# Batched x·yᵀ in float32: tile 0 leaves PSUM in two separate halves, loads and tiles take other slots, and tiles 2 to 5 leave as pairs

## The chip, the cores and the metric

The kernel runs on one core of one Trainium2 chip. The metric is the device time of one execution in microseconds (us); the kernel before has a median of 297.6 us over three runs (297.5 to 297.63). Engines are called PE (matrix products), DVE (VectorE), ACT (ScalarE), POOL (GpSimd) and SP (SyncE, which here only issues transfers). Transfers between HBM and on-chip memory (SBUF) are moved by 16 DMA engines.

## The reference

```python
def setup_inputs():
    batch, n_heads, seq_t, seq_s, channels = 8, 12, 512, 512, 64
    ...
def reference(x, y):
    return np.einsum('bhtc,bhsc->bhts', x, y).astype(np.float32)
```

For each of the 96 heads, a 512 x 64 matrix times a transposed 512 x 64 matrix gives a 512 x 512 matrix. The inputs are 25.2 MB and the output is 100.7 MB, all float32.

## The kernel before

**Tiles.** The 96 heads form six groups of 16. A *load* brings one group of x or of y, 2 MB, into one slot of SBUF: 128 partitions by 16 KB. There are twelve loads; load n is x of group n/2 for even n and y for odd n. A *result tile* is two heads of output, also 2 MB and also one slot; there are 48, four to each half group. The buffer `room` holds eight slots. Loads use slots 0 to 4; slots 5 to 7 at first hold bf16 copies of groups 1 to 3 and serve as result slots once these have been used.

**Stages.** `compress(n)` turns a landed load into bf16: an x load by one ACT cast of about 3.6 us; a y load by four casts of quarters, two on DVE, one on POOL, one on ACT (for the last y load none on ACT). `mix` (POOL for the first three half groups, DVE later) puts x in a layout padded with zeros, and `transposes` (DVE) makes the operands xT and yT of a half group. PE then computes a tile as two *halves*, each four matmuls into one of two PSUM buffers `pm0` and `pm1`; ACT copies each half from PSUM into the tile's slot ("evicts" it, 128 x 2048 values), which frees that PSUM buffer for PE. When both halves are in the slot, SP issues the store to HBM.

**Order.** The order on each engine is that of the program, written by hand in the loop over n at line 430 and the loop over tiles at line 446. Every engine works strictly through its own list, and `emit` puts the semaphore waits in front of each instruction. SP's list matters here: it holds all loads and stores, so a load or store behind a waiting one waits too. Loads 0 to 4 are issued first, loads 5 to 9 after `compress(0..4)`, load 10 after `compress(6)` and load 11 after `compress(8)`. `result(o)` (line 390) evicts the two halves of tile o and calls `store(o)` (line 365). Tile 0 comes after `compress(8)`, tile 1 after `compress(9)`, tile 2 after `compress(10)`, tile 3 before `compress(11)`, and the others after the loop.

**Slots and stores.** Line 154 (`places`) gives the slot of each load, line 155 (`alone`) that of the first six tiles (`SINGLE`), which are stored one by one at line 382: 2 MB each, read as 16 KB from each partition. From tile 6 on, two tiles lie in adjacent slots and are stored by one transfer of 4 MB at line 386, read as 32 KB from each partition. `ROUNDS` lists which pair of slots each such store uses: three pairs in turn for the first ten, then four. The last four tiles have a special arrangement (`shares`, `rest`): part of tile 44 is stored in small pieces, some of them from POOL's queue, and a part of it is computed again at the very end.

**Waits on a slot.** A tile may be evicted into a slot once the previous store from it has landed, or, for a slot that held a load, once all casts have read it. Slots 5 to 7 also wait for the readers of the bf16 copies there (`held`).

Of the kernel before, what the change touches and what calls it, by code (L numbers as in the profile page):

```python
# [9 lines left out]
def kernel(  # L10
# [25 lines left out]
    NH = 2 * NG  # L36
    V = G // 4
    K = 8
# [1 line left out]
    D = 32  # L40
    SLOTS = 5
    N = K * S
    SINGLE = 2 * V - 2
    SHARED = V * NH - V
    PAIRS = 4
    LATE = 10
    ROUND = [1, 0, 2]
    ROUNDS = [ROUND[n % 3] for n in range(LATE)]
    while len(ROUNDS) < (V * NH - SINGLE) // 2:
        ROUNDS += [PAIRS - 1, *ROUND[LATE % 3:], *ROUND[:LATE % 3]]  # L50
    LAST = 2 * ROUNDS[(V * NH - SINGLE) // 2 - 1]
    CUT = [S, 3 * S]
    LEFT = 2 * S
    fp32 = mybir.dt.float32
# [8 lines left out]
    ov = of.rearrange("(o u h q n) -> o h q u n", u=2, h=V, q=Q * E, n=N)  # L63
    ow = of.rearrange("(o a j q n) -> o j q a n", a=4, j=2, q=Q * E, n=N)

    def buffer(name, width, dtype):
        return nc.alloc_sbuf_tensor(name, [P, width], dtype)[:, :]

    room = buffer("room", 2 * PAIRS * N, fp32)
    pairs = [room[:, 2 * n * N:2 * (n + 1) * N] for n in range(PAIRS)]  # L70
    slots = [p[:, j * N:(j + 1) * N] for p in pairs for j in range(2)]

    def spare(g, lo, hi):

# [24 lines left out]
    def need(name, points, told=True):  # L99

        best = {}
        for p, v in points:
            if known[name].get(p, 0) < v:
                best[p] = max(best.get(p, 0), v)
        for p, v in list(best.items()):
            if any(snaps[q, w].get(p, 0) >= v for q, w in best.items() if q != p):
                del best[p]
        for p, v in best.items():
            if told:
                engines[name].wait_ge(sems[p], v)  # L110
            known[name][p] = v
            for q, w in snaps[p, v].items():
                known[name][q] = max(known[name].get(q, 0), w)
# [20 lines left out]
    def signal(p):  # L134
        if p not in sems:
            sems[p] = nc.alloc_semaphore(p)
        return sems[p]

    def emit(name, make, reads=(), writes=(), dma=None, by=None, step=1):
        need(name, promise(name, reads, writes))  # L140
        p = by or name
        if dma is not None:
            p, step = f"dma{dma}", 16
        made = make().then_inc(signal(p), step)
        record(name, p, step, reads, writes, dma is not None)
        return made.ins.name


    late = [f"dma{LAST}", "dmapool"]
    for p in late:  # L150
        signal(p)
    loaded = {}

    places = [0, 1, 2, 3, 4, 0, 1, 2, 3, 4, 1, 3]
    alone = [0, 2, 4, 0, 1, 4]
    heads = [0, 2, 1, 3]
    held = {
        SLOTS + g - 1: [[("xk", g)], [("yb", h, g, ch) for h in range(2) for ch in range(2)]]
# [15 lines left out]
    def both(*ids):  # L174
        return [("slot", i, pm) for i in ids for pm in range(2)]

    def place(ap, pattern):
        name = ap.tensor.name
        return mybir.PhysicalAccessPattern(
            ap=pattern, offset=ap.offset, dtype=ap.dtype, memref=name, memsetref=f"{name}_set"  # L180
        )

    def transfer(name, dst, src, to=None, of=None):

        to = to or dst.ap
        of = of or [src.ap[0], *[[1, 1]] * (len(to) - len(src.ap)), *src.ap[1:]]
        return engines[name].add_instruction(  # L187
            mybir.InstDMACopy(
                name=nc.get_next_instruction_name(),
                engine=engines[name].engine,  # L190
                ins=[place(src, of)],
                outs=[place(dst, to)],
                mode="Copy",
                cce_op=mybir.AluOpType.bypass,
                queue={"sp": "qSPDynamicHW", "pool": "qPoolDynamic"}[name],
            )
        )
# [48 lines left out]
    def transposes(i):  # L246
        g, half = divmod(i, 2)
        b = g % (NG - 1 + half)
        emit(
            "dve",  # L250
            lambda: nc.vector.transpose(  # L251
                xTs[half].rearrange("p (k r e) -> p k e r", k=K, e=E),
                xbs[half].rearrange("p (k e c) -> p k e c", k=K, e=E),
            ),
            [("xb", half, part) for part in range(4)],
            [("xT", half)],
        )
        emit(
            "dve",
            lambda: nc.vector.transpose(  # L260
                yTs[half].rearrange("p (r j) -> p j r", r=D),
                ybs[half][b].rearrange("p (j c) -> p j c", c=D),
            ),
            [("yb", half, b, ch) for ch in range(2)],
            [("yT", half)],
            by="made",
            step=V,
        )
# [23 lines left out]
    def part(name, dst, src, k, reads, dma):  # L292

        assert src.ap[0][1] == 2 * k and dst.ap[0][1] == k
        emit(
            name, lambda: transfer(name, dst, src, dst.ap),
            reads=reads, dma=dma,
        )

    def shares(o, s):  # L300

        to, mine = ov[o // V, heads[o % V]], slots[s]
        def odd(name, b, e, k, lo, hi):

            p = 4 * e + 32 * b + (32 if e > 7 else 0)
            n = 2 * k
            dst = to[p // 2:p // 2 + n, 1, lo:hi].rearrange("(k i) n -> k i n", i=2)
            part(name, dst, mine[p + 1:p + 2 * n:2, lo:hi], k, both(s), "pool" if name == "pool" else s)

        for b in range(2):  # L310
            for e, k in turns:
                odd("pool", b, e, k, 0, N if e else CUT[b])
        for b in range(2):
            odd("sp", b, 0, 4, CUT[b], N - b * LEFT)
# [35 lines left out]
    def rest():  # L350
# [7 lines left out]
        for b, first, width, n, e, k, skip in sorted(remade, key=lambda r: r[4]):  # L358
# [3 lines left out]
            p = lies(e)  # L362
            part("pool", dst, mine[p + 1:p + 4 * k:2, skip:skip + width], k, [("xk", 0)], "pool")

    def store(o):
        i, j = divmod(o, V)
        if o == SHARED:
            s = 2 * ROUNDS[(o - SINGLE) // 2]
            shares(o, s)
        elif o == SHARED + 1:  # L370
            n = ROUNDS[(o - SINGLE) // 2]
            emit(
                "sp", lambda: transfer("sp", ow[i, heads[j - 1]][:, :2], pairs[n][::2]),
                reads=both(2 * n, 2 * n + 1), dma=2 * n,
            )
            emit(
                "sp", lambda: transfer("sp", ov[i, heads[j]][:, 1], slots[2 * n + 1][1::2]),
                reads=both(2 * n + 1), dma=2 * n + 1,
            )
        elif o < SINGLE:  # L380
            s = alone[o]
            emit("sp", lambda: nc.sync.dma_start(ov[i, heads[j]], slots[s]), reads=both(s), dma=s)
        elif o % 2:
            n = ROUNDS[(o - SINGLE) // 2]
            emit(
                "sp", lambda: transfer("sp", ow[i, heads[j - 1]], pairs[n]),
                reads=both(2 * n, 2 * n + 1), dma=2 * n,
            )

    def result(o):  # L390

        s = alone[o] if o < SINGLE else 2 * ROUNDS[(o - SINGLE) // 2] + o % 2
        ot = slots[s].rearrange("p (r s) -> p r s", s=S)
        for k in range(0, K, 4):
            pm = k // 4
            half = o // V % 2
            reads, writes = [("xT", half), ("yT", half)], [("pm", pm)]
            signal("pe")
            need("pe", promise("pe", reads, writes), told=False)
            record("pe", "pe", 1, reads, writes)  # L400
            copy(
                "dve" if o == V * NH - 1 else "act", ot[:, k:k + 4, :], pms[pm],
                [("pm", pm)], [("slot", s, pm), *(held[s][pm] if s in held else ())], by=f"free{pm}",
            )
        store(o)

    def prepare(i):

        if i < NH:
            transposes(i)  # L410
        if i + 1 < NH:
            for part in range(4):
                mix(i + 1, "dve", part)
# [14 lines left out]
            writes=[("xb", half, part) for part in range(4)],  # L428
        )
    for n in range(2 * NG):  # L430
        if n == 11:
            result(3)
        compress(n)
        mix(n // 4, "pool", n % 4)
        if n == 4:
            transposes(0)
        if n < 5:
            load(n + SLOTS)
        elif n in (6, 8):
            load(n // 2 + 7)  # L440
        if n > 7 and n < 11:
            result(n - 8)
        if n == 9:
            transposes(1)
    prepare(2)
    for o in range(V, V * NH):
        result(o)
        if o % V == V - 1:
            prepare(o // V + 2)
# [39 lines left out]
```

## Time and profile before

The median is 297.6 us. The profiled execution took 297.78 us, of which the core's span from first to last instruction is 296.0 us; 1.78 us lie around it.

| view | value |
|---|---|
| DMA, hardware queue, share of 16 engines over the span | 98.7% |
| bytes moved, mean rate | 125.85 MB, 425 GB/s |
| ACT busy | 205.2 us (69%) |
| DVE busy | 157.5 us (53%) |
| PE busy | 138.5 us (47%) |
| POOL busy | 64.7 us (22%) |
| ACT, eviction of half a tile | 1.89 us each, 94 of them |
| ACT, cast of an x load | 3.62 us |
| ACT, cast of a quarter of a y load | 2.45 us |
| single store, 2048 KB, issue to landing | 11.0 us median |
| pair store, 4096 KB, issue to landing | 24.3 us median |

The time from issue to landing counts the time that a transfer stands behind earlier ones in the queue. An engine's idle time costs the kernel nothing while the DMA engines have work; what costs is a moment in which the queue of transfers is empty.

### The profile page before, as it was taken

How to read it: one execution, taken by the hardware profiler on the slowest of the kernel's cores; microseconds unless marked ns; L12 is line 12 of the kernel's file. 1: busy time of each engine (PE TensorE's matmuls, PEld its weight loads, DVE VectorE, ACT ScalarE, POOL GpSimd, SP SyncE). 2: the span in 40 equal slices, each digit the busy share in tenths (PEclk: the TensorE clock that was granted, in tenths of full speed). 3: DMA queues.
4: the chain of work that ended last, by engine and by line, in shares of the span. 5: the costliest groups of instructions: out<-in, count | busy, mean ns of one | idle time of the engine just before them, and what ended most of it. 6: DMA issues, size and time to landing. Idle time of an engine off the chain costs nothing.

```text
span 296.0 us, 1222 instructions
## 1 busy us (share of the span) xinstructions
PE 138.5 (47%) x403; PEld 37.6 (13%) x403; DVE 157.5 (53%) x76; ACT 205.2 (69%) x106; POOL 64.7 (22%) x33
## 2 busy tenths in 40 slices
PE   0000040558576556557644856567646646674000
PEld 0000010112121111111111211111111111121000
DVE  2257897996969591925908568772925100052000
ACT  1665676999799979666966999969666976640000
POOL 2399989996000000000000000000000000402000
PEclk9999995556779995778789599975798786757555
DMA  7999999999999999999999999999999999999998
GB/s 283 425 432 430 427 432 427 432 427 430 430 434 447 425 426 443 438 443 443 425 425 422 425 425 438 447 434 443 430 425 425 425 425 434 424 424 453 409 422 354
DMA packets 6042, 125.85 MB, mean 425 GB/s; under 512 B 952, under 2 KB 952, under 8 KB 996
## 3 DMA queue, kind: packets, MB, share of 16 engines
q1 hardware_dynamic: 5656, 124.95, 98.7%
q0 software_dynamic: 384, 0.89, 0.8%
q14 instruction: 2, 0.02, 0.0%
HBM read 25.17 MB, written 100.66 MB: 425 GB/s over the span
## 4 chain that ended last, share of the span: by engine, by line
DMA 52%; ACT 25%; PE 6%; issue 5%; DVE 3%; POOL 1%; SPq 0%; ACTq 0%
DMA out_dram<-room 38%; ACT room L166 24%; DMA room<-in_y_dram 7%; DMA room<-in_x_dram 6%; PE pm L274 4%; DVE room L168 3%; PE pm L343 2%; ACT xk L166 1%; ACT yb L166 1%; POOL out_dram L187 1%; DVE xk L168 0%; SPq L203 0%; ACTq L110 0%
## 5 line engine op out<-in xcount | busy, mean ns | idle before, releaser
L274 PE MATMUL pm<-yT,xT 128*128 128x512 bf16 x384 | 133.6, 492 | 130.6 <-ACT room L166 93.9
L166 ACT ACTIVATE room<-pm 128x2048 f32<-128x2048 f32 x94 | 170.1, 1891 | 35.0 <-DMA out_dram<-room 31.8
L251 DVE STREAM_TRANSPOSE xT<-xb 128x2048 uint32<-128x2048 uint32 x12 | 46.7, 3895 | 59.6 <-PE pm L274 54.9
L274 PEld LDWEIGHTS pm<-yT,xT 128*128 128x128 bf16 x384 | 35.3, 113 | 228.0 <-ACT room L166 148.2
L187 POOL DMA_DIRECT2D out_dram<-room x6 | 3.5, 590 | 180.8 <-ACT room L166 180.8
L168 DVE COPY xb<-room 32x2048 bf16<-32x2048 bf16 x20 | 26.1, 1304 | 0.6
L166 ACT ACTIVATE room<-room 128x4096 bf16<-128x4096 f32 (+1 forms) x6 | 18.2, 3039 | 11.1 <-DMA room<-in_x_dram 7.3
L168 POOL COPY xb<-xk 32x2048 bf16<-32x2048 bf16 x8 | 23.5, 2937 | 6.7 <-ACT xk L166 6.3
L168 DVE CAST yb<-room 64x2048 bf16<-64x2048 f32 x6 | 17.1, 2853 | 9.5 <-DMA room<-in_y_dram 9.5
L168 DVE COPY room<-pm 128x2048 f32<-128x2048 f32 x2 | 4.5, 2286 | 31.9 <-PE pm L274 31.9
L168 DVE CAST room<-room 64x2048 bf16<-64x2048 f32 x6 | 19.0, 3170 | 4.1 <-DMA room<-in_y_dram 4.0
L168 DVE COPY xb<-xk 32x2048 bf16<-32x2048 bf16 x16 | 20.9, 1304 | 0.4
L166 ACT ACTIVATE xk<-room 128x4096 bf16<-128x4096 f32 x3 | 10.8, 3617 | 5.5 <-DMA room<-in_x_dram 5.4
L168 POOL CAST yb<-room 64x2048 bf16<-64x2048 f32 x4 | 12.8, 3188 | 0.5 <-DMA room<-in_y_dram 0.2
L168 POOL COPY xb<-room 32x2048 bf16<-32x2048 bf16 x4 | 12.7, 3180 | 0.3
L260 DVE STREAM_TRANSPOSE yT<-yb 128x1024 uint32<-128x1024 uint32 x6 | 11.6, 1940 | 0.0
L260 DVE STREAM_TRANSPOSE yT<-room 128x1024 uint32<-128x1024 uint32 x6 | 11.4, 1906 | 0.0
L168 POOL CAST room<-room 64x2048 bf16<-64x2048 f32 x3 | 8.5, 2837 | 1.0 <-DMA room<-in_y_dram 0.7
L166 ACT ACTIVATE yb<-room 64x2048 bf16<-64x2048 f32 x2 | 4.9, 2454 | 1.3 <-DMA room<-in_y_dram 1.3
L343 PE MATMUL pm<-yT,xT 128*84 128x512 bf16 (+17 forms) x19 | 5.0, 442 | 0.6 <-DVE room L168 0.6
L187 POOL DMA_DIRECT2D out_dram<-xk x3 | 1.7, 571 | 15.2 <-DVE xk L168 15.2
L427 DVE MEMSET xb<- 128x2048 uint32 x1 | 1.8, 1765 | 4.5 <-PEq L419 4.5
(8 smaller groups left out, 7.0 us busy)
## 6 DMA issues: line engine op xcount, KB each, us to landing
out_dram<-room SPq DMA_DIRECT2D x20, 4096.0 KB, 24.3
out_dram<-room SPq DMA_DIRECT2D x7, 2048.0 KB, 11.0
room<-in_x_dram SPq DMA_DIRECT2D x6, 2048.0 KB, 18.6
room<-in_y_dram SPq DMA_DIRECT2D x6, 2048.0 KB, 20.8
out_dram<-room SPq DMA_DIRECT2D x1, 1024.0 KB, 29.4
out_dram<-room POOLq DMA_DIRECT2D x2, 256.0 KB, 18.4
out_dram<-room POOLq DMA_DIRECT2D x2, 96.0 KB, 16.4
out_dram<-room SPq DMA_DIRECT2D x1, 112.0 KB
```

What stands on the lines that cost most here:

```text
L166: lambda: nc.scalar.activation(dst, src, COPY)
L168: else engines[name].tensor_copy(dst, src),
L187: return engines[name].add_instruction(mybir.InstDMACopy(name=nc.get_next_instruction_name(), engine=engines[name].engine, ins=[place(src, ...
L251: lambda: nc.vector.transpose(xTs[half].rearrange("p (k r e) -> p k e r", k=K, e=E), xbs[half].rearrange("p (k e c) -> p k e c", k=K, e=E),),
L260: lambda: nc.vector.transpose(yTs[half].rearrange("p (r j) -> p j r", r=D), ybs[half][b].rearrange("p (j c) -> p j c", c=D),),
L274: last = nc.tensor.matmul(pms[k // 4][:, j, :], xT[:, k + j, h, :], yT[:, h * S:(h + 1) * S], start=True, stop=True,)
L343: last = nc.tensor.matmul(pms[0][:top, at // S, at % S:at % S + hi - lo], xT[:, stop - top:stop], yT[:, h * S + lo % S:h * S + lo % S + hi ...
L427: lambda: engines[name].memset(xbs[half], 0.0),
```

## The change

- **Tile 0 in halves.** `result` is split: `evict(o, ...)` copies the named halves, and `result` calls it for both and then `store`. Half 0 of tile 0 is now evicted before ACT's cast of `compress(7)` and half 1 after it. Its store is issued after `compress(8)` and load 11. Tile 1 follows at once after `compress(8)`, and tiles 2 and 3 both after `compress(10)`.
- **Slots.** Loads and tiles get other slots. For the loads this is a renaming (slot 1 becomes 3, 2 becomes 1, 3 becomes 2). `home(o)` gives a tile's slot: tiles 0 and 1 in slots 0 and 1, the pairs then from the list `FIRST` of first slots: 3, 0, 2, then 4, 0, 2 repeated, then 6, 4, 0, 2 repeated.
- **Pairs.** `SINGLE` falls from 6 to 2, so tiles 2 and 3 leave as one store of 4 MB, and tiles 4 and 5 as another. There are 28 large stores (tiles 0 and 1, and pairs) where there were 30, before the special arrangement of tiles 44 and 45. Tiles 26 and 27 are the first in slots 6 and 7, as before.

```diff
-    SINGLE = 2 * V - 2
+    SINGLE = 2
...
-    LATE = 10
-    ROUND = [1, 0, 2]
-    ROUNDS = [ROUND[n % 3] for n in range(LATE)]
-    while len(ROUNDS) < (V * NH - SINGLE) // 2:
-        ROUNDS += [PAIRS - 1, *ROUND[LATE % 3:], *ROUND[:LATE % 3]]
-    LAST = 2 * ROUNDS[(V * NH - SINGLE) // 2 - 1]
+    LATE = 12
+    FIRST = [3, 0, 2, *[4, 0, 2] * 3]
+    while len(FIRST) < (V * NH - SINGLE) // 2:
+        FIRST += [6, 4, 0, 2]
+    LAST = FIRST[(V * NH - SINGLE) // 2 - 1]
...
-    places = [0, 1, 2, 3, 4, 0, 1, 2, 3, 4, 1, 3]
-    alone = [0, 2, 4, 0, 1, 4]
+    places = [0, 3, 1, 2, 4, 0, 3, 1, 2, 4, 3, 2]
...
+    def home(o):
+        return o if o < SINGLE else FIRST[(o - SINGLE) // 2] + o % 2
+
     def store(o):
         i, j = divmod(o, V)
+        s = home(o)
+        pair = room[:, (s - 1) * N:(s + 1) * N]
...
         elif o < SINGLE:
-            s = alone[o]
             emit("sp", lambda: nc.sync.dma_start(ov[i, heads[j]], slots[s]), reads=both(s), dma=s)
         elif o % 2:
-            n = ROUNDS[(o - SINGLE) // 2]
             emit(
-                "sp", lambda: transfer("sp", ow[i, heads[j - 1]], pairs[n]),
-                reads=both(2 * n, 2 * n + 1), dma=2 * n,
+                "sp", lambda: transfer("sp", ow[i, heads[j - 1]], pair),
+                reads=both(s - 1, s), dma=s - 1,
             )
-    def result(o):
-        s = alone[o] if o < SINGLE else 2 * ROUNDS[(o - SINGLE) // 2] + o % 2
+    def evict(o, *pms_of):
+        s = home(o)
         ot = slots[s].rearrange("p (r s) -> p r s", s=S)
-        for k in range(0, K, 4):
-            pm = k // 4
+        for pm in pms_of:
+            k = 4 * pm
...
+    def result(o):
+        evict(o, 0, 1)
         store(o)
...
     for n in range(2 * NG):
-        if n == 11:
-            result(3)
+        if n == 7:
+            evict(0, 0)
         compress(n)
         mix(n // 4, "pool", n % 4)
...
-        if n > 7 and n < 11:
-            result(n - 8)
-        if n == 9:
+        if n == 7:
+            evict(0, 1)
+        elif n == 8:
+            store(0)
+            result(1)
+        elif n == 9:
             transposes(1)
+        elif n == 10:
+            result(2)
+            result(3)
```

More of the change, by code (lines that the diff above doesn't have):

```diff
@@ L42 @@
     N = K * S
-    SINGLE = 2 * V - 2
+    SINGLE = 2
     SHARED = V * NH - V
     PAIRS = 4
-    LATE = 10
-    ROUND = [1, 0, 2]
-    ROUNDS = [ROUND[n % 3] for n in range(LATE)]
-    while len(ROUNDS) < (V * NH - SINGLE) // 2:
-        ROUNDS += [PAIRS - 1, *ROUND[LATE % 3:], *ROUND[:LATE % 3]]
-    LAST = 2 * ROUNDS[(V * NH - SINGLE) // 2 - 1]
+    LATE = 12
+    FIRST = [3, 0, 2, *[4, 0, 2] * 3]
+    assert len(FIRST) == LATE
+    while len(FIRST) < (V * NH - SINGLE) // 2:
+        FIRST += [6, 4, 0, 2]
+    LAST = FIRST[(V * NH - SINGLE) // 2 - 1]
     CUT = [S, 3 * S]
@@ L69 @@
     room = buffer("room", 2 * PAIRS * N, fp32)
-    pairs = [room[:, 2 * n * N:2 * (n + 1) * N] for n in range(PAIRS)]
-    slots = [p[:, j * N:(j + 1) * N] for p in pairs for j in range(2)]
+    slots = [room[:, n * N:(n + 1) * N] for n in range(2 * PAIRS)]
     def spare(g, lo, hi):
@@ L363, in rest @@
             part("pool", dst, mine[p + 1:p + 4 * k:2, skip:skip + width], k, [("xk", 0)], "pool")
+    def home(o):
+        return o if o < SINGLE else FIRST[(o - SINGLE) // 2] + o % 2
     def store(o):
         i, j = divmod(o, V)
+        s = home(o)
+        pair = room[:, (s - 1) * N:(s + 1) * N]
         if o == SHARED:
-            s = 2 * ROUNDS[(o - SINGLE) // 2]
             shares(o, s)
         elif o == SHARED + 1:
-            n = ROUNDS[(o - SINGLE) // 2]
             emit(
-                "sp", lambda: transfer("sp", ow[i, heads[j - 1]][:, :2], pairs[n][::2]),
-                reads=both(2 * n, 2 * n + 1), dma=2 * n,
+                "sp", lambda: transfer("sp", ow[i, heads[j - 1]][:, :2], pair[::2]),
+                reads=both(s - 1, s), dma=s - 1,
             )
             emit(
-                "sp", lambda: transfer("sp", ov[i, heads[j]][:, 1], slots[2 * n + 1][1::2]),
-                reads=both(2 * n + 1), dma=2 * n + 1,
+                "sp", lambda: transfer("sp", ov[i, heads[j]][:, 1], slots[s][1::2]),
+                reads=both(s), dma=s,
             )
         elif o < SINGLE:
-            s = alone[o]
             emit("sp", lambda: nc.sync.dma_start(ov[i, heads[j]], slots[s]), reads=both(s), dma=s)
         elif o % 2:
-            n = ROUNDS[(o - SINGLE) // 2]
             emit(
-                "sp", lambda: transfer("sp", ow[i, heads[j - 1]], pairs[n]),
-                reads=both(2 * n, 2 * n + 1), dma=2 * n,
-            )
-    def result(o):
-        s = alone[o] if o < SINGLE else 2 * ROUNDS[(o - SINGLE) // 2] + o % 2
+                "sp", lambda: transfer("sp", ow[i, heads[j - 1]], pair),
+                reads=both(s - 1, s), dma=s - 1,
+            )
+    def evict(o, *pms_of):
+        s = home(o)
         ot = slots[s].rearrange("p (r s) -> p r s", s=S)
-        for k in range(0, K, 4):
-            pm = k // 4
+        for pm in pms_of:
+            k = 4 * pm
             half = o // V % 2
```

## The prediction

> **What bounds the kernel now.** I read the slices of the page first, then the DMA queues, then windows.
>
> ```profile
> DMA  7999999999999999999999999999999999999998
> GB/s 283 425 432 430 427 432 427 432 427 430 430 434 447 425 426 443 438 443 443 425 425 422 425 425 438 447 434 443 430 425 425 425 425 434 424 424 453 409 422 354
> q1 hardware_dynamic: 5656, 124.95, 98.7%
> 62.00:90.00 28.00, 17.72 (x50) 4.49 (x48) 22.55 (x11) 25.92 (x15) 9.46 (x4) 0.72 1.01 431
> 90.00:250.00 160.00, 96.56 (x288) 25.69 (x288) 87.75 (x49) 129.74 (x73) 0.00 (x0) 0.82 1.01 433
> ```
>
> The DMA row is full from the second slice to the last but one: the DMA engines never run dry, at 430 GB/s. No compute engine is above 69%. So the end moves only if bytes move at another rate, or if the queue of transfers becomes empty for a moment. In the last two lines (last column GB/s, before it the DMA share) the stage of single stores, 62 to 90 us, moves 431 GB/s and the stage of pairs 433.
>
> The change works between 41 and 90 us, so I read ACT's and DVE's timelines there (start, length, what), and SP's.
>
> ```profile
> 36.34 13.70 DVE L168 CAST room<-room 64x2048 bf16<-64x2048 f32 x4
> 42.64 2.44 ACT L166 ACTIVATE room<-room 64x2048 bf16<-64x2048 f32 x1 [1.27 <-DMA room<-in_y_dram]
> 47.55 3.62 ACT L166 ACTIVATE xk<-room 128x4096 bf16<-128x4096 f32 x1 [2.46 <-DMA room<-in_x_dram]
> 51.07 3.63 ACT L166 ACTIVATE room<-pm 128x2048 f32<-128x2048 f32 x2
> 54.72 2.46 ACT L166 ACTIVATE yb<-room 64x2048 bf16<-64x2048 f32 x1
> 57.21 3.65 ACT L166 ACTIVATE room<-pm 128x2048 f32<-128x2048 f32 x2
> 60.88 3.62 ACT L166 ACTIVATE xk<-room 128x4096 bf16<-128x4096 f32 x1
> 64.41 3.63 ACT L166 ACTIVATE room<-pm 128x2048 f32<-128x2048 f32 x2
> 68.25 7.18 ACT L166 ACTIVATE room<-pm 128x2048 f32<-128x2048 f32 x4 [0.21 <-PE pm L274]
> ...
> 68.06 8.74 DMA out_dram<-room
> ...
> 88.26 0.54 SPq L187 DMA_DIRECT2D out_dram<-room  x1
> ...
> 0.74 0.38 SPq L203 DMA_DIRECT2D room<-in_x_dram  x1
> ```
>
> The reader sees the casts of loads 7 to 10 (42.64, 47.55, 54.72, 60.88) and between them tiles 0, 1, 2 (51.07, 57.21, 64.41), tile 3 first in the line at 68.25. ACT idles 1.27 us before load 7's cast and 2.46 before load 8's. Tile 2's store is issued at 68.06 and lands at 76.79. The first pair, tiles 6 and 7, is issued at 88.26.
>
> **When the queue would be empty.** Loads land every 4.90 us (the starts 42.64 and 47.55), and single stores take 2.097 MB / 431 GB/s = 4.87 us, so tile 1's store lands at 76.79 - 4.87 = 71.92. The trace's packet records are finer: the 16 engines move the last bytes of tile 1's store between 70.98 and 71.48, mean 71.23, about half a microsecond before landing. Behind tile 1 the queue now holds tile 2; after the change it holds the pair of tiles 2 and 3, which can be issued only when tile 3 has been evicted.
>
> **Part 1, ACT's new order.** Half 0 of tile 0 goes to slot 0, which held load 5; its last reader is the second of the four DVE casts that start at 36.34, which ends at 43.13. PE has the half ready at 38.5 (tile 0's eight matmuls run from 36.59 to 40.18). So ACT, free at 41.37, starts at 43.2 and from there has no wait for a load: load 8 has landed by 47.5, load 9 by 52.4, load 10 by 57.4 (4.90 after load 9). Steps by start-to-start distance in ACT's rows: half tile then cast 1.89; cast of load 7 2.49; half tile 1.89; cast of load 8 3.52; tile 1 3.67; cast of load 9 2.49; cast of load 10 3.52; tile 2 3.63; wait for PE 0.21 as in the row at 68.25 (PE at half clock, 0.50 in that stage); tile 3 3.64. Sum 26.95: tile 3 is complete at 70.15 instead of 71.89, and the pair is issued at 70.18. If PE has the full clock, the 0.21 goes: 69.97.
>
> What waits behind the two moved halves: load 7's ACT cast ends 2.46 us later, but its result is needed only by the transposes of half group 7. Load 8's cast ends at 53.1 instead of 51.16, and with it load 11 is issued at 53.1 instead of 51.19, ahead of tile 0's store in SP's list. The engines finish load 10 at 56.36 to 56.85, a lead of 3.2 us; the pair at 88.26 had a lead of 2.17 over the end of tile 5's bytes (90.43) and its landing shows no gap, so 3.2 is safe. Without that cover each us would be a us of the end. Tile 0's store (issue 53.5 instead of 54.72) and tile 1's (56.7 instead of 60.88) have leads of 8 and 9 us. DVE and POOL keep their order. These edits cost nothing.
>
> **Part 2, slots.** Tile 4 goes to slot 0 (store landed 67.1) and tile 5 to slot 1 (71.93): ACT does them from 70.0 to 77.3, issue 77.3, while the first pair keeps the queue busy to about 81; lead 3.9. Tile 7 needs slot 3, free when that pair lands near 82; pair 6-7 issued at 86, lead 5. Tile 9 goes to slot 5, two tiles earlier than any tile used it; it needs the transposes of half group 3 on DVE, which can start when PE ends tile 7 (about 82.8) and last 3.9 + 1.9: 88.6, against ACT at tile 9's second half at about 91. Free by 2.5 us. From there three pairs rotate, then four, as before; the tail is the same with slots 0, 1 and 4, 5 exchanged. All this costs nothing while those leads stand; beyond them, a us of lateness is a us of the end.
>
> **Part 3, reads of 32 KB.** Two pairs take the place of four single stores: 8.39 MB at 433 instead of 431 GB/s, 19.37 instead of 19.46 us: **-0.09 us**. Bounds: pairs land 9.79 to 9.82 us apart (ACT's starts 111.39, 121.18, 130.98; 140.76, 150.56), two loads take 9.80, so the least is 0; the 2 GB/s is good to about one, so the most is -0.15.
>
> **Part 4, the queue at 71 us.** The pair is issued at 70.18 with a lead of 0.80 to 1.30 us. The trace shows an empty queue only once, at the start: issue at 0.74 (0.38 long), first packet at 1.755, all 16 engines by about 2.2, mean 1.2 after the issue; then the 194 packets of the first 10 us take 0.687 us on average instead of 0.612, which is 0.075 x 194 / 16 = 0.91 us per engine lost in coming up to speed. By the start's delay the engines get the pair at 71.39 on average, idle 0.16; a store's issue is 0.16 longer (0.54), which gives 0.32. I take the middle, 0.24. The loss in coming up lies between 0 (an engine that is not dry has none) and 0.91 (reads from HBM into a system at rest). I take a third, 0.3, since these reads are from SBUF and the pause is short, so it lies nearer the running queue. Sum **0.54 us**, bounds 0 and 0.32 + 0.91 = 1.23.
>
> **Sum.** -0.09 + 0.54 = +0.45 us. The DMA queue is full from there to the end, so it carries through: 297.78 + 0.45 = 298.23 for the profiled execution, which was 0.18 above the median; on the median 298.05, say **298.0 us**. Bounds 297.45 (no gap, -0.15) and 298.83 (1.23, gain 0).
>
> **Rivals.**
> - *The gap is hidden.* The issue is ahead of the dry point by 0.80 to 1.30; if an issue needs less than that while the queue runs, no engine stops. For it: 2.17 sufficed. Against: the only delay in the trace is 1.02 to the first packet. Time 297.6 - 0.09 = 297.5. The Trainium skill ("DMA: Bandwidth & Descriptors", Specifications) gives about 0.6 us to the first byte on this path, an issue at 70.18 then delivering at 70.8, before 70.98: by that rule the time is 297.5. The trace agrees with 0.6 only if it counts from the end of the issue (1.12 to 1.755).
> - *Slower: the pause costs the whole start-up.* Place: the pair of tiles 2 and 3 at 71 us. Price as at the start, 0.32 + 0.91 = 1.23, less 0.09: 298.7. It decides (over 0.2%, 0.6 us) from a gap of 0.69 us on; 0.15 us more on ACT's chain of ten steps adds the same again. For it: the only empty queue on record cost that. Against: SBUF reads, engines dry only in part.
> - *Each transfer has a fixed price.* Two stores fewer would then save more than 0.6 us: below 297.0. Against: one pair store lands 9.80 after the other and two loads take the same 9.80, so a queued transfer pays nothing. The Trainium skill (same page, "Anatomy of one DMA") fits 2.0 us plus the bytes per DMA for GpSimd's path; two such prices less would give an estimate of 293.5, which the equal distances in the trace speak against.
>
> **How the numbers follow.** Partial gap 0.43 (a tenth of that above 0.69), hidden 0.17, whole start-up 0.36, fixed price 0.04. Within 0.2% (0.6 us, about what a measurement of this kernel can tell from no change) is 0.39 + 0.17 = 0.56, slower 0.40, faster 0.04. The range leaves out the fixed price and the outer end of the start-up: 297.4 to 298.8. Forecast's own range: 297.8 to 298.4.
>
> **What would show it.** Tile 0's halves at 43.2 and 47.6 on either side of a cast; ACT without a wait of over 0.1 us from 43.2 to 66; load 11 issued at 53.1; the pair of tiles 2 and 3 issued near 70.2 and, in narrow windows from 70 to 74 us, a DMA rate below 400 GB/s; pair 4-5 issued near 77.3 with no gap behind it. Wrong it is if ACT waits elsewhere (slot 0 later than 43.2, tile 9 for DVE), or if the rate never falls at 71 us.

## The result, and the profile after

The changed kernel takes **299.0 us** (median of 6 runs, 298.87 to 299.24) against 297.62 for the kernel before: the ratio is **1.0044, 95% interval 1.0031 to 1.0057**. It is slower by 1.4 us, above the range of the prediction (297.4 to 298.8). The profiled execution of the changed kernel took 298.93 us with a span of 297.1 us, against 297.78 and 296.0: 1.15 us apart, where the medians are 1.4 apart.

ACT's timeline in the changed kernel (start, length, what, and in brackets the wait before it), then the issues of SP that follow tile 3 and tile 5 ("SPq" is SP's queue of transfers):

```profile
43.26 1.88 ACT L166 ACTIVATE room<-pm 128x2048 f32<-128x2048 f32 x1 [1.86 <-DVE room L168]
45.16 2.47 ACT L166 ACTIVATE room<-room 64x2048 bf16<-64x2048 f32 x1
47.66 1.88 ACT L166 ACTIVATE room<-pm 128x2048 f32<-128x2048 f32 x1
49.56 3.62 ACT L166 ACTIVATE xk<-room 128x4096 bf16<-128x4096 f32 x1
...
62.96 3.65 ACT L166 ACTIVATE room<-pm 128x2048 f32<-128x2048 f32 x2
66.81 14.27 ACT L166 ACTIVATE room<-pm 128x2048 f32<-128x2048 f32 x8 [0.21 <-PE pm L274]
...
70.48 0.54 SPq L187 DMA_DIRECT2D out_dram<-room  x1
...
77.56 0.54 SPq L187 DMA_DIRECT2D out_dram<-room  x1
```

The reader sees the two halves of tile 0 on either side of a cast, tiles 2 and 3 at the end, and the first pair issued at 70.48 (forecast 70.18). Now the DMA engines in windows of half a microsecond (the last two columns are the DMA share, by packets that start in the window, and GB/s), first the kernel before, then the changed one:

```profile
70.50:71.00 0.50, 0.50 (x2) 0.15 (x1) 0.00 (x0) 0.50 (x1) 0.50 (x1) 0.50 0.92 393
71.00:71.50 0.50, 0.50 (x3) 0.15 (x1) 0.00 (x0) 0.50 (x1) 0.50 (x1) 0.88 1.17 492
71.50:72.00 0.50, 0.22 (x2) 0.06 (x2) 0.22 (x1) 0.50 (x2) 0.25 (x1) 1.00 1.00 426
72.00:72.50 0.50, 0.50 (x3) 0.25 (x4) 0.50 (x1) 0.50 (x1) 0.00 (x0) 1.00 0.92 393
```

```profile
70.50:71.00 0.50, 0.49 (x3) 0.25 (x4) 0.00 (x0) 0.50 (x1) 0.50 (x1) 1.00 0.99 426
71.00:71.50 0.50, 0.50 (x3) 0.06 (x1) 0.00 (x0) 0.50 (x1) 0.50 (x1) 1.00 0.02 0
71.50:72.00 0.50, 0.05 (x1) 0.00 (x0) 0.20 (x1) 0.50 (x1) 0.27 (x1) 1.00 2.43 1049
72.00:72.50 0.50, 0.22 (x1) 0.11 (x2) 0.50 (x1) 0.50 (x2) 0.00 (x0) 1.00 0.00 0
```

In the kernel before every window moves 393 GB/s or more. In the changed one no packet of data starts from 71.0 to 71.5, and then all 16 engines start within one window. (The zero of the last row is no stand: a packet of 32 KB counts where it starts, and all 16 are under way.) So the forecast gap is there. It is not the whole loss. The packet records of the trace tell when each of the 16 engines ends its share of a store, since each share closes with a packet of 4 bytes. The mean of these 16 ends, in us:

```
                                  before    changed   difference added
end of tile 1's store              71.23      71.27    +0.04
end of tiles 2 and 3               80.97      81.52    +0.51   the stand and the restart
end of the 17 pairs that follow   245.98     247.25    +0.72   9.689 -> 9.743 a pair up to 160 us
end of the special last stores    295.05     296.49    +0.17
last engine over the mean          +0.47      +0.17    -0.30
last engine                       295.52     296.66    +1.14
```

(Before, "17 pairs" are tiles 4 and 5 as two single stores, and 16 pairs.) The *stand*, the time in which the engines have nothing to move, cost 0.51 us together with the restart, close to the forecast. Behind it **every pair took about 0.05 us more up to 160 us, and 0.03 more later**. This *pace*, the time for 4 MB, is the part that the prediction had not. (The difference shrinks because the kernel before, in this execution, goes from 9.689 to 9.711 us a pair at about 170 us; the kernel of run 6 below, which is the same up to 236 us, goes to 9.697 only.) The slower pace is hardly to be seen in the page's own rows: 425 and 424 GB/s over the span, 98.7% and 98.6% of the 16 engines.

```profile
DMA packets 6042, 125.85 MB, mean 425 GB/s; under 512 B 952, under 2 KB 952, under 8 KB 996
q1 hardware_dynamic: 5656, 124.95, 98.7%
```

```profile
DMA packets 5754, 125.85 MB, mean 424 GB/s; under 512 B 920, under 2 KB 920, under 8 KB 964
q1 hardware_dynamic: 5368, 124.95, 98.6%
```

These are the page's DMA lines of before and after: the same bytes in 288 fewer packets.

### The profile page after: what moved, and what is told of

Its sections match the earlier page's. It is cut to its first block, busy times and chain, and to the rows that moved or that the text cites. A ratio compares the mean times of both kernels' runs of the same rounds, so it can differ in the third digit from the quotient of the medians.

```text
span 297.1 us, 1219 instructions
## 1 busy us (share of the span) xinstructions
PE 136.9 (46%) x403; PEld 37.0 (12%) x403; DVE 157.7 (53%) x76; ACT 205.5 (69%) x106; POOL 64.7 (22%) x33
## 3 DMA queue, kind: packets, MB, share of 16 engines
q1 hardware_dynamic: 5368, 124.95, 98.6%
## 4 chain that ended last, share of the span: by engine, by line
DMA 47%; ACT 22%; POOL 7%; DVE 6%; PE 5%; issue 3%; ACTq 0%; POOLq 0%
DMA out_dram<-room 45%; ACT room L166 18%; DVE room L168 5%; PE pm L274 4%; POOL xb L168 4%; ACT xk L166 3%; DMA room<-in_x_dram 3%; POOL room L168 1%; POOL yb L168 1%; PE pm L343 1%; ACT yb L166 1%; DVE yT L260 1%; POOL out_dram L187 1%; DVE xk L168 0%; ACTq L110 0%
```

## The experiments

The first theory: the engines stand at 71 us because the pair is issued too late, and start again together; in step, they are slower. Its rival: the new slots and pairs set the slower pace, and the stand costs only its own half microsecond. All values called *stand* and *pace* below are means over the 16 engines from the packet records of one profiled execution of each kernel. A stand is given as the time by which the store behind it takes longer than a store of its size did before, so it includes the first slow packets; the pace is the median of the intervals between ends of pairs from 100 to 160 us. Diffs are shortened where "..." stands.

**1. Take the lateness away, by ACT.** One cast of load 9 goes from ACT to DVE.

```diff
-                    in_front[2 * half + ch] if n < 2 * NG - 1 or ch == 0 else "pool",
+                    ("dve" if n == 9 and half == 1 else in_front[2 * half + ch]) if n < 2 * NG - 1 or ch == 0 else "pool",
```

> The changed kernel, with ACT's quarter cast of load 9 given to DVE (same work, another engine), so that ACT reaches tile 3 about 2.5 us earlier and the pair of tiles 2 and 3 is issued near 68.0 instead of 70.5. Theory (a pause at 71 us, and after it a slower pace because the 16 DMA engines restart in step): no pause, so no slow pace either: a pair takes 9.69 to 9.72 us, time 297.4 to 297.7. Rival (the new slots and pairs set the slower pace, the pause only its own half microsecond): no pause, but a pair still takes 9.74, time about 297.5 + 17 x 0.04 = 298.2.

Measured: **297.6 us, ratio 0.9995 (0.9986 to 1.0004)**. ACT and SP:

```profile
57.35 3.62 ACT L166 ACTIVATE xk<-room 128x4096 bf16<-128x4096 f32 x1 [0.62 <-DMA room<-in_x_dram]
61.06 3.65 ACT L166 ACTIVATE room<-pm 128x2048 f32<-128x2048 f32 x2
...
68.59 7.63 SPq L187 DMA_DIRECT2D out_dram<-room  x2
```

The cast of load 10 now follows tile 1 with a short wait for the load, and the pair is issued at 68.59, 2.4 us before the first engine ends tile 1. No stand, pace 9.695. All slots and pairs of the change are in this kernel, so the rival falls: they do not set the slower pace.

**2. Take the lateness away, by the store.** Tiles 2 and 3 are stored singly again; all else stays as changed.

```diff
-        elif o < SINGLE:
+        elif o < SINGLE or o in (2, 3):
```

> The changed kernel, with tiles 2 and 3 stored one by one (2 MB each) as before; all else of the change stays, the slots, the halves of tile 0 and the pair of tiles 4 and 5. Tile 2 is then issued near 66.6, four us before the queue is dry. Theory: no pause, pace 9.69 to 9.72, time 297.4 to 297.7. Rival (slots and order set the pace): pace 9.74, time 298.2 to 298.4.

Measured: **297.57 us, ratio 0.9993 (0.9984 to 1.0003)**, no stand, pace 9.694. Its windows at the place of the stand:

```profile
71.00:71.50 0.50, 0.50 (x3) 0.10 (x1) 0.00 (x0) 0.50 (x1) 0.50 (x1) 1.00 1.16 492
71.50:72.00 0.50, 0.12 (x1) 0.00 (x0) 0.08 (x1) 0.50 (x1) 0.38 (x1) 1.00 1.23 524
```

Against run 1 this also prices the 32 KB reads: tiles 2 and 3 end 9.735 us after tile 1 as single stores and 9.691 as a pair, so a pair saves 0.044 us and two save 0.09.

**3. The lateness alone, in the kernel before.** Tile 2's store also waits for both halves of tile 3.

```diff
+        elif o == 2:
+            pass
         elif o < SINGLE:
+            if o == 3:
+                t = alone[2]
+                emit("sp", lambda: nc.sync.dma_start(ov[0, heads[2]], slots[t]),
+                    reads=both(t) + both(alone[3]), dma=t)
...
```

> The kernel before, its slots and stores unchanged, but tile 2's store also waits for both halves of tile 3: issued at 71.9 instead of 68.1. With 1.2 us from issue to first packet the engines stand from 71.2 to 73.1, 1.9 us on average. Theory: the pause costs 1.9, and the restart in step slows each later pair to 9.74: 297.6 + 1.9 + about 0.7 = 300.2. Rival (slots and pairs of the change set the pace): pace stays 9.69 to 9.71, time 299.5.

Measured: **300.59 us, ratio 1.0099 (1.0083 to 1.0114)**. SP's issue of tile 2's store:

```profile
72.01 0.54 SPq L386 DMA_DIRECT2D out_dram<-room  x1
```

The stand is 2.10 us, and the pace 9.745. About 0.8 us of the loss of 2.9 come after the stand, with the old slots and stores: the slow pace belongs to the lateness. The time is 0.4 us above the theory's 300.2.

**4. A shorter wait: the first half of tile 3 only** (`[("slot", alone[3], 0)]` in place of `both(alone[3])`).

> The kernel before, but tile 2's store also waits for the first half of tile 3: issued at 70.2 instead of 68.1, 0.8 to 1.3 us before the engines have moved the last of tile 1. Theory (1.2 us from issue to first packet, then the restart in step): the engines stand 0.2 to 0.3 us on average and are drawn closer together; pace 9.71 to 9.74, time 298.1 to 298.5. Rival (an issue ahead of the dry queue costs nothing, only a queue that is dry at the issue does): no pause, 297.6.

Measured: **298.87 us, ratio 1.0038 (1.0024 to 1.0051)**. SP's issue and the window of the stand:

```profile
70.20 0.54 SPq L386 DMA_DIRECT2D out_dram<-room  x1
...
71.50:72.00 0.50, 0.00 (x0) 0.00 (x1) 0.17 (x1) 0.50 (x2) 0.29 (x1) 1.00 0.23 98
```

The issue comes 0.8 us ahead of the first engine that runs dry (has moved its last byte). The stand is 0.27 us, of which 0.20 without a packet, and the pace is the full slow one, 9.742. In all this costs 1.1 us, more than the theory's 0.5 to 0.9.

**5. A still earlier issue, at 69.6.** Tile 2's store waits for DVE's second cast of load 11.

```diff
-        store(o)
+        if o not in (2, 3):
+            store(o)
...
         compress(n)
+        if n == 11:
+            store(2, [("yb", 1, NG - 1, 0)])
+            store(3)
```

> The kernel before, but tile 2's store waits for DVE's second cast of load 11: issued at 69.5 instead of 68.1, 1.5 to 2.0 us before the engines have moved the last of tile 1. Theory (an issue needs 1.2 to 1.35 us to the first packet, and any stand of the engines, however short, costs the slower pace): no stand, pace 9.69 to 9.71, 297.5 to 297.9. Rival (the lead has to be over 2 us, since the first descriptors of the later engines come later): a stand of 0.1 us and the slow pace, 298.5 to 298.8.

Measured: **298.43 us, ratio 1.0029 (1.0018 to 1.0040)**. SP and the windows:

```profile
69.61 6.52 SPq L382 DMA_DIRECT2D out_dram<-room  x3
...
71.00:71.50 0.50, 0.35 (x2) 0.00 (x0) 0.00 (x0) 0.50 (x1) 0.50 (x1) 1.00 1.01 426
71.50:72.00 0.50, 0.00 (x0) 0.00 (x0) 0.11 (x1) 0.50 (x2) 0.36 (x1) 1.00 1.23 524
72.00:72.50 0.50, 0.42 (x2) 0.21 (x3) 0.50 (x1) 0.50 (x2) 0.00 (x0) 1.00 1.08 459
```

The rate does not fall. The engines go from tile 1's last packet to tile 2's first within 0.007 us on average, as they do in the kernel before, so there is no stand; tile 2's store ends 4.879 us after tile 1's instead of 4.867. The 16 ends still lie 0.50 us apart, as before. And yet the pace drifts off: 4.873, 4.874, 4.890 a tile, then 9.72 to 9.77 a pair. So an issue 1.4 us ahead of the first dry engine is too late, though nothing stands. The theory, which gave 297.5 to 297.9, fails here, and so does "in step": these engines are not in step.

**6. The stand late in the kernel.** The kernel before, with the store of tiles 36 and 37 held back until tile 41 is complete.

```diff
...
+        if o in (37, 39):
+            return
+        if o == 41:
+            store(37, both(s))
+            store(39)
         store(o)
```

> The kernel before, but the store of tiles 36 and 37 also waits for tile 41 and is issued with the stores of 38/39 and 40/41, at 236.6 instead of 217.0, when most engines have been dry since about 236. First packets at 237.8: a stand of 1.7 us, 160 us later than in the changed kernel. Theory (stand plus 0.03 to 0.05 us for each pair that follows): 297.7 + 1.7 + 4 pairs and the tail, 0.2 = 299.6 (299.3 to 299.9). Rival (a stand has a fixed price of 0.8 us besides its length): 300.2 to 300.6.

Measured: **299.07 us, ratio 1.0050 (1.0034 to 1.0066)**. The pace is 9.689 up to 160 us and 9.697 from there to the stand; the windows at the stand:

```profile
235.00:236.00 1.00, 0.77 (x3) 0.05 (x1) 0.00 (x0) 1.00 (x1) 0.00 (x0) 0.78 0.31 131
236.00:237.00 1.00, 0.84 (x4) 0.31 (x4) 0.00 (x0) 0.11 (x1) 0.00 (x0) 1.00 0.08 33
237.00:238.00 1.00, 0.20 (x1) 0.00 (x0) 0.00 (x0) 0.00 (x0) 0.00 (x0) 1.00 1.24 524
```

The pair takes 11.049 instead of 9.697, a stand of 1.35 us (1.7 was expected, since the issue came at 236.13, not 236.6). The loss of 1.49 us is little more than that. At 71 us a stand of 0.27 cost 1.1 (run 4). So a stand has no fixed price beside its length; the rest is the pace of the pairs behind it, and here there are few.

**7 to 9. Small extra stores that move the engines apart.** Rows of tile 47's place are stored early, some engines getting more than others; tile 47's own store writes over them. Run 7 has seven stores (14, 12, ... 2 rows of 2 KB), run 8 three (12, 8, 4 rows of 4 KB), run 9 one (8 rows of 16 KB), all behind the pair of tiles 2 and 3:

```diff
+            if o == 3:
+                for n in (12, 8, 4):
+                    dst = ov[NH - 1, heads[V - 1]][:n, 0, 256 * n:256 * n + 1024]
+                    emit("sp", lambda: transfer("sp", dst, slots[s][:n, :1024]),
+                        reads=both(s), writes=[("early", n)], dma="x")
...
```

> The changed kernel, with seven small extra stores behind the pair of tiles 2 and 3: 14, 12, 10, ... 2 rows of 2 KB (one row on each of as many DMA engines) into tile 47's place, which tile 47's own store writes over at the end. They cost an engine 0 to 0.56 us, 0.28 on average, and leave the engines that far apart. Theory: the pause stays, but the pace returns to 9.69 to 9.72 per pair; time 299.0 + 0.28 - 0.6, so 298.4 to 299.0. Rival (slots and pairs set the pace): pace stays 9.74, time 299.3 to 299.6.

> The changed kernel, with three small extra stores behind the pair of tiles 2 and 3 (12, 8 and 4 rows of 4 KB, one row on each of as many DMA engines, into tile 47's place, which tile 47's own store writes over at the end). The pause at 71 us stays. The engines are then about 0, 0.16, 0.31 and 0.47 us apart in groups of four, and the next pair is still issued at 77.8, before the queue is dry. Theory (the pace is set by how many engines start their packets together): pace back to 9.69 to 9.71 per pair, time about 299.0 + 0.3 - 16 x 0.04 = 298.6. Rival (something else that the pause leaves behind, or the slots): pace stays 9.74, time 299.3 to 299.5.

> The changed kernel, with one extra store of 8 rows of 16 KB behind the pair of tiles 2 and 3 (one row on each of eight DMA engines, 0.61 us each; into tile 47's place, which tile 47's own store writes over at the end). The stand at 71 us stays; eight engines are then half a packet behind the other eight. Theory (the pace follows from how many engines start a packet together): pace 9.70 to 9.72, at least for the first pairs. Rival (what counts is which neighbours start together, the small stores moved the pace by another way): pace 9.74. The time is 299.0 + 0.3 to 0.9 for the store, less 0 to 0.6.

Measured: 300.85 us (ratio 1.0102, 1.0086 to 1.0117), 300.69 (1.0099, 1.0084 to 1.0115) and 301.54 (1.0131, 1.0115 to 1.0147). All three lie above both forecasts. Run 7 decides nothing: SP needed 0.9 to 1.4 us to issue each small store, the next pair was issued at 80.5 to 82.6 and the queue ran dry a second time; pace 9.745. Runs 8 and 9 had no second stand: pace 9.714 and 9.724 up to 160 us, and 9.74 after 170 us, with the engines' starts as far apart then as before. That is part of the way back, for a time, and at a cost that the bytes do not explain: the next pair ends 0.9 us later for 0.1 MB in run 8 and 1.2 later for 0.13 MB in run 9, with the engines then 1.9 and 2.7 us apart. Distance between the engines can't be the whole matter.

**10. A small store with no lateness.** The kernel before, with one extra store of 8 rows of 4 KB behind tile 3.

```diff
+            if o == 3:
+                dst = ov[NH - 1, heads[V - 1]][:8, 0, :1024]
+                emit("sp", lambda: transfer("sp", dst, slots[s][:8, :1024]),
+                    reads=both(s), writes=[("early", 8)], dma="x")
...
```

> The kernel before, with one extra store of 8 rows of 4 KB behind tile 3 (one row, 0.16 us, on each of eight DMA engines; into tile 47's place, which tile 47's own store writes over at the end). No engine stands for want of a transfer, all else is the kernel before. Theory (any upset of how the engines lie to each other costs pace, with or without a stand): pace 9.71 to 9.74 per pair instead of 9.69, time 297.6 + 0.2 + 0.5 = 298.3 (298.0 to 298.8). Rival (only a queue that runs dry upsets it): pace 9.69, time 297.7 to 297.9.

Measured: **297.7 us, ratio 1.0002 (0.9992 to 1.0012)**, pace 9.689. It delays half of the engines by a packet of 4 KB, and the pace does not mind. The form of the theory by which any upset costs pace falls, as the rival had it.

**11 and 12. Something full-width behind the stand: a load, or a store.** The changed kernel with 0.25 MB over all 16 engines behind the late pair, once as a load of x into an unused buffer, once as a store into tile 47's place.

```diff
+            if o == 3:
+                emit("sp", lambda: nc.sync.dma_start(spot, xv[0][:, :512]), writes=[("spot", 0)], dma="x")
```

```diff
+            if o == 3:
+                emit("sp", lambda: nc.sync.dma_start(ov[NH - 1, heads[V - 1]][:, :, :512], slots[s][:, :512]),
+                    reads=both(s), writes=[("early", 0)], dma="x")
...
```

> The changed kernel, with one extra load of 2 KB for each of the 128 partitions (0.25 MB, 0.6 us of the engines) into an unused buffer behind the pair of tiles 2 and 3. In every run so far the engines lie 0.4 to 0.7 us apart after the one place where loads give way to stores (61 us), whatever they were before, and take 4.87 us a tile from there. Theory (the lasting pace comes from how the engines lie relative to each other, which the stand at 71 us upset): passing from a load to a store again may set it right: pace 9.69 to 9.71, time 299.0 + 0.6 - 0.7 = 298.9. Rival (the stand leaves something that engine order does not mend): pace 9.74, time 299.6 or more.

> The changed kernel, with one extra store of 2 KB from each of the 128 partitions behind the pair of tiles 2 and 3 (0.25 MB on all 16 engines, like the extra load that brought the pace back to 9.69, but in the direction of the stores; into tile 47's place, which tile 47's own store writes over at the end). Theory A (it was the load, passing from reading HBM to writing it again): pace stays 9.74, time 299.0 + 0.6 = 299.6. Theory B (any short transfer over all 16 engines shifts them out of the bad pattern): pace 9.69, time 299.0 + 0.6 - 0.7 = 298.9.

Measured: both 299.66 us (ratios 1.0070, 1.0053 to 1.0087, and 1.0066, 1.0049 to 1.0083). The times are equal, but the pace is not. Behind the load it is **9.689**, exactly that of the kernel before; behind the store it is **9.743**, as in the changed kernel. The load costs more than it brings: with the late pair, whose own share rises from 10.25 to 10.88 us, and its 0.65 us it takes 1.27 us more than the pair alone. The faster pace wins back about 0.5 us of this up to 160 us, and from 170 us on it goes to 9.74 again, with no late issue there. The engines' ends lie only 0.25 us apart behind the load, closer than in the kernel before (0.84 behind the first pair), and they are fast. With run 5 (apart and slow) this ends the "in step" form of the theory.

What the packet records do show in each kernel is the time of a single 32 KB packet, here of those that start from 106 to 155 us:

```
kernel                               pace    packets of 1213 or 1214 ns   mean ns
before                               9.689        95%                     1214.1
cast of load 9 on DVE (run 1)        9.695        94%                     1214.8
load behind the stand (run 11)       9.689        94%                     1214.2
issue 1.4 us ahead (run 5)           9.735        32%                     1219.7
three small stores (run 8)           9.714        59%                     1217.3
changed                              9.743        17%                     1220.8
store behind the stand (run 12)      9.743        17%                     1221.1
```

In the fast kernels nearly every packet takes the same time to a nanosecond. In the changed kernel five of six lie anywhere from 1213 to 1222, and 42 of 641 are past 1240 (7 of 652 before). The pace is not one state of all engines, either. The trace does not name a packet's engine, but a packet begins within some 10 ns of the end of the one before it on its engine, so the 16 chains can be followed (where engines lie within a few ns, two may be mixed up). The number of regular engines, with 90% or more of their packets at 1213 or 1214 ns:

```
kernel              90-106   130-155   180-205   205-234 us
before                 15        15        10         8
run 1                  15        14        15        15
run 5                   4         3         1         1
run 8                  10         5         1         1
run 11                 15        15         2         1
changed                 0         1         1         1
```

One engine is irregular even in the fastest kernel. In the others more and more become so, one after another, and the paces between 9.69 and 9.74 are such mixtures. In the kernel before and in run 11 this happens after 160 us with every store issued over 9 us ahead, so a late issue is not the only thing that brings it on. What makes an engine irregular, and why a load in between ends it for a time, these runs do not settle.

## Why the prediction was wrong

- **What bounds the kernel:** right. The end moved with the DMA engines alone; ACT, DVE and PE have the same busy times in both profiles within 2 us.
- **Part 1:** right in its mechanism, 0.3 us short. Tile 0's halves came at 43.26 and 47.66, load 11 was issued at 53.20, tile 3 was complete at 70.46 instead of 70.15. Of the 0.3, 0.06 is there at the start and 0.19 comes before tile 2 (62.96 instead of 62.67): load 10's cast and tile 2 start 3.71 us apart, not 3.52. The new slots fit this, though no run tests it: tile 2 now goes to slot 3, which held load 10, so it has to wait until that cast has ended.
- **Part 2:** right. The pair of tiles 4 and 5 was issued at 77.56, and no other stand shows.
- **Part 3:** right, 0.09 us by runs 1 and 2.
- **Part 4:** near in the sum by luck, wrong in its halves. The engines had no packet for 0.47 us (0.24 taken) and lost only about 0.1 in coming up to speed (0.3 taken); less the 0.04 that one pair saves, that is the 0.51 of the table, against 0.54. The 0.24 was good for the issue that it was worked out for: run 4, issued at 70.20, had 0.20 us without a packet. The rest of the 0.47 is the 0.30 of Part 1. The delay taken from the kernel's start holds here too: in run 3 the first packet came 1.19 us after the issue at 72.01.
- **The sum is the step that failed:** "The DMA queue is full from there to the end, so it carries through". The queue was full, as it says, but a full queue was taken for an unchanged rate, and the rate had changed: +0.72 us over the next 17 pairs and +0.17 in the tail's mean, less 0.30 since the last engine is nearer to the mean. Runs 3 and 4 show the slow pace with the old slots and stores, runs 1 and 2 the fast pace with the new slots: the late issue sets it off. By what mechanism stays open.
- **"The pair at 88.26 had a lead of 2.17 ... and its landing shows no gap":** right for that lead, and the pace behind it stayed 9.69. What a shorter lead does was guessed: 1.4 us sufficed to keep the engines moving and not to keep the pace (run 5); 2.4 us sufficed for both (run 1).
- **Rivals.** *Hidden* is excluded by the window without a packet. The first packet came 1.20 us after the issue, 0.66 after its end at 71.02. The 0.6 us of the Trainium skill ("DMA: Bandwidth & Descriptors", Specifications) agrees here if it is counted from the end of the issue. *Whole start-up* gave 298.7, near the measured 299.0, by a cause that was not there: the loss came later, over 170 us. *Fixed price of a transfer*, at some 0.3 us or more a store, is excluded by run 2 against run 1: two single stores take only 0.044 us more than one pair.

## What to carry to other kernels

When transfers bound a kernel, merging two stores makes the first of them wait for the second: compare its new issue time with the moment at which the engines run dry, and want some 2 us between them here, not just a positive number (1.4 was too little, 2.2 enough). A short stand early costs more than its length, because the pace behind it can change too; price it by the pairs that follow. Where a page shows the same share and nearly the same GB/s, compare the intervals between ends of equal transfers, which tell half a per cent apart.

## What the runs showed of the hardware

- The stores of this kernel run at 9.69 to 9.74 us for 4 MB, with all transfers queued ahead, depending on how many of the 16 engines move their 32 KB packets in an even 1213 to 1214 ns. A late issue brings on the slow end, also without a stand (run 5). A load of 0.25 MB behind it brought the fast end back up to 160 us (run 11), and a store of the same size did not (run 12). Each is read from one profiled execution.
- From an issue on SP to the first packet of a queue run dry it took 1.20 us for a store (70.48 to 71.68; in runs 3 and 4, 1.19 and 1.20).
- Stores of a few rows are dear on SP: 0.8 to 1.4 us to issue 2 to 14 rows, against 0.54 for 4 MB. In a full queue one of 8 rows cost nothing that could be measured (run 10); behind a stand the engines lost about four times what the bytes take at the usual rate (runs 8 and 9), which stays unexplained.
- No version beat the kernel before by what can be told apart: with a cast moved to DVE, or with tiles 2 and 3 stored singly, the change is worth 0.9995 (0.9986 to 1.0004) and 0.9993 (0.9984 to 1.0003).
